# First mixer of a hybrid encoder: u's first block between the gate's two groups, LayerNorm's factor and shift behind the token mix, 1/sqrt for three blocks at once

## The chip, the cores and the metric

The kernel runs on one core of one Trainium2 chip. The metric is the time of one execution on the device, in microseconds (us); lower is better. The core has TensorE (matrix products, PE in the profile; its weight loads are PEld), VectorE (DVE), ScalarE (ACT), GpSimd (POOL) and SyncE (SP, which here issues nearly all transfers). They run side by side and wait for each other by semaphores.

## The reference

A trunk of two layers is applied to two token groups (512 and 256 tokens, width 1024) with shared weights. Layer 0 is half a SwiGLU block, a mixer, half a SwiGLU block; layer 1 the same with another mixer; a final RMSNorm follows. The change touches the mixer of layer 0:

```python
def layer_norm(x, g, b):
    x32 = x.astype(jnp.float32)
    mu = jnp.mean(x32, axis=-1, keepdims=True)
    var = jnp.mean(jnp.square(x32 - mu), axis=-1, keepdims=True)
    y = (x32 - mu) * lax.rsqrt(var + EPS)
    return y.astype(x.dtype) * g + b

def mixer_ab(h, w_in, sgu_ln_g, sgu_ln_b, sgu_w, sgu_b, sink, w_out):
    z = h @ w_in
    zs = jax.nn.gelu(z[..., :1024], approximate=False)
    u, vh = zs[..., :512], zs[..., 512:]
    vh = layer_norm(vh, sgu_ln_g, sgu_ln_b)
    vh = vh.reshape(B, nc, 128, 4, 128)
    vmix = jnp.einsum('gij,bnjgc->bnigc', sgu_w, vh) + jnp.transpose(sgu_b)[None, None, :, :, None]
    a_out = u * vmix.reshape(B, L, 512)
    ...
    b_out = window_gqa(rope_partial(q), rope_partial(k), v, sink)
    return jnp.concatenate([a_out, b_out], axis=-1) @ w_out
```

What is left out takes q, k and v from the other columns of z. So u is the multiplying half, vh the gate; the gate is normalised over its 512 columns for each token, mixed over the 128 tokens of a block with one matrix for each group of columns, and multiplied with u.

## The kernel before, in words

All 768 tokens are worked on together. The activations lie with the model's columns on partitions: eight tiles of 128 x 768. To keep float32 accuracy each operand of a product is split in a high part (a cast to fp32r, on ScalarE, `split` and `wsplit`, L193 and L111) and a low part (the rest, on VectorE, L194 and L112), and each product is three matmuls (`mm3`). Weights come in pieces of 512 KB through four "raw" buffers; a piece is split into "whi" and "wlo" tiles of 512 columns, of which there are five each (`NW`). PSUM is used as two pools of four banks: "mm" for projections, "aux" for all else.

The order on TensorE is written out by the program; the other engines' orders are planned when the kernel is built, by readiness and program order. What has to wait for other engines is written as generators ("chains"): each `yield x` says that the next step is due when x microseconds of matmul work, by the program's own count `self.t`, have been put behind it, and `tick` after every `mm3` runs the steps that are due. `drain` runs a chain to its end at once. So TensorE's order is fixed, and where a step's operand isn't ready TensorE stands still.

In `mixer0` (L916 and on) come, in this order: loads of tables; projections of keys and values; `attention` as a chain (12 units of scores, exps, transposes and products with the values, `score`, `turn`, `values`; L878, L883, L892, L141, L1051, L1055); query projections 0 to 2 (`q_heads`, with the rotation `roped`, L952 to L955); `vh_part`; query projection 3; `u_part`; and `mixer_out`, the output projection.

`vh_part` computes the gate in two groups of three token blocks, tokens on partitions, 512 columns on the free side, three "mm" banks at once; after a group three gelus (L1123) write "vg" tiles and a chain `sgu` is spawned for each block. `sgu` takes the statistics (L1084, L1087), forms 1/sqrt by `rsqrt` (13 operations on one column, L258 to L269), normalises (L1089), multiplies by g and adds b (L1092 and L1093, with both spread over the partitions); 8, 11 or 14 us later it splits (vhh, vhl), 4 us later it issues 12 matmuls for the token mix into an "aux" bank and adds the bias (L1107), which leaves the result with columns on partitions in the tiles `ot`. `u_part` takes u's columns in four blocks of 128: projection for 512 and for 256 tokens, scaling (L1133), gelu (L1134), and the product with `ot` (L1137); in front of the first product all `sgu` chains are drained.

The tag "tmp" has three buffers of 128 x 512; the gate's vg tiles, u's tiles, the rotation's two (rt, ru), vf and the attention's copy tb (L1051) share them. Gelu and exp are in different tables of ScalarE, so that a load (ACT_TABLE_LOAD) stands between them.

Of the kernel before, what the change touches and what calls it, by code (L numbers as in the profile page):

```python
# [21 lines left out]
TA, TB = 512, 256  # L22
T = TA + TB
H = T // 2
GROUPS = ((0, TA), (TA, T))
# [24 lines left out]
class Trunk:  # L50
# [864 lines left out]
    def mixer0(self):  # L915
        nc = self.nc  # L916
        mp = self.mixer_open("m0")
        self.spawn(self.norm_r(mp, False))
        xs = (self.xh, self.xl)
        tmp = lambda name: mp.tile([P, TA], F32, tag="tmp", name=name, bufs=3)  # L920
        rct = mp.tile([P, T], F32, tag="rct", name="rct")
        rst = mp.tile([P, T], F32, tag="rst", name="rst")
        for t, i in ((rct, 0), (rst, 1)):
# [5 lines left out]
        nc.sync.dma_start(sink, self.aps["sink"].partition_broadcast(P))  # L929
        nsink = mp.tile([P, 8], F32, tag="nsink", name="nsink")  # L930
        nc.vector.tensor_scalar(out=nsink, in0=sink, scalar1=-1.0, scalar2=None, op0=ALU.mult)
        lng = mp.tile([P, 512], F32, tag="lng", name="lng")
        nc.sync.dma_start(lng, self.aps["ln_g"].partition_broadcast(P))
        lnb = mp.tile([P, 512], F32, tag="lnb", name="lnb")
        nc.sync.dma_start(lnb, self.aps["ln_b"].partition_broadcast(P))
        sb = mp.tile([P, 512], F32, tag="sb", name="sb")
        nc.sync.dma_start(sb, self.aps["sgu_b"].partition_broadcast(P))
        swr = tmp("swr")
# [1 line left out]
        swh = mp.tile([P, 4, P], F32R, tag="swh", name="swh")  # L940
        swl = mp.tile([P, 4, P], F32R, tag="swl", name="swl")
        self.split(swh.rearrange("p g j -> p (g j)"), swl.rearrange("p g j -> p (g j)"), swr)
        swap = [i ^ 8 if i < 16 else i for i in range(32)]

        def rope_tables():
            for t in (rct, rst):
                nc.vector.tensor_tensor(out=t, in0=t, in1=self.rt, op=ALU.mult)
# [25 lines left out]
        for g in (0, 1):  # L973
            c0, c1 = GROUPS[g]
            t = roped(pkv[g][0], c0, c1)
# [3 lines left out]
                out=vf[:, : c1 - c0], in0=pkv[g][1][:, : c1 - c0], in1=self.rt[:, c0:c1], op=ALU.mult  # L979
# [3 lines left out]
        ot = [self.otile(k) for k in range(KD)]  # L983
# [73 lines left out]
                        in0=po[0:64, c], in1=tb[:, c], op=ALU.add,  # L1057
                    )

        qheads, gates = [], []  # L1060

        def attention(gap):
            cur = None
# [14 lines left out]
            yield 1.0  # L1078
            values(*cur, tt)

        def sgu(n, v):

            bs = mp.tile([P, 6], F32, tag="bs", name="bs", bufs=2)
            nc.vector.bn_stats(out=bs, in_=v)  # L1084
            mv = mp.tile([P, 8], F32, tag="mv", name="mv", bufs=2)
            it = mp.tile([P, 1], I32, tag="mvi", name="mvi", bufs=2)
            nc.vector.bn_aggr(out=mv[:, 0:2], in_=bs)  # L1087
            self.rsqrt(mv[:, 2:3], mv[:, 1:2], 1.0, mv[:, 3:4], mv[:, 4:5], it)
            nc.vector.tensor_scalar(  # L1089
                out=v, in0=v, scalar1=mv[:, 0:1], scalar2=mv[:, 2:3], op0=ALU.subtract, op1=ALU.mult  # L1090
            )
            nc.vector.tensor_tensor(out=v, in0=v, in1=lng, op=ALU.mult)  # L1092
            nc.vector.tensor_tensor(out=v, in0=v, in1=lnb, op=ALU.add)  # L1093
            yield SGU[0] + n % 3 * SGU[1]
            vh = mp.tile([P, 512], F32R, tag="vhh", name="vhh", bufs=2)
            vl = mp.tile([P, 512], F32R, tag="vhl", name="vhl", bufs=2)
            self.split(vh, vl, v)
            yield SGU[2]
            ps = self.psum(self.aux, "aux")
            for g in range(4):  # L1100
                c = slice(g * P, (g + 1) * P)
                self.mmul(ps[:, c], vh[:, c], swh[:, g, :], True, False)
                self.mmul(ps[:, c], vh[:, c], swl[:, g, :], False, False)
                self.mmul(ps[:, c], vl[:, c], swh[:, g, :], False, True)
            for g in range(4):
                c = slice(g * P, (g + 1) * P)
                nc.vector.tensor_tensor(  # L1107
                    out=ot[g][:, n * P : (n + 1) * P], in0=ps[:, c], in1=sb[:, c], op=ALU.add
                )

        def vh_part():
            for n0 in (0, 3):
                ps = [self.psum() for _ in range(3)]
                for k in range(KD):
                    if k % 2 == 0:
                        w = self.unit("l0_w_in", k, 2, 512, 512)
                    for i in range(3):
                        a, b = (n0 + i) * P, (n0 + i + 1) * P
                        st = (self.xh[k][:, a:b], self.xl[k][:, a:b])
                        self.mm3(ps[i], st, w[k % 2], k == 0, k == KD - 1)  # L1120
                for i in range(3):
                    v = tmp("vg")
                    nc.scalar.activation(v, ps[i], AF.Gelu, scale=self.ry[:, n0 + i : n0 + i + 1])  # L1123
                    gates.append(self.spawn(sgu(n0 + i, v)))

        def u_part():
            for m in range(4):
                w = self.unit("l0_w_in", 0, KD, m * P, P)
                for g in (0, 1):
                    c0, c1 = GROUPS[g]  # L1130
                    ps = self.proj(w, xs, GROUPS[g])
                    u = tmp("ug")[:, : c1 - c0]
                    nc.vector.tensor_tensor(out=u, in0=ps[:, : c1 - c0], in1=self.rt[:, c0:c1], op=ALU.mult)  # L1133
                    nc.scalar.activation(u, u, AF.Gelu)  # L1134
                    for c in gates:
                        self.drain(c)
                    nc.vector.tensor_tensor(out=ot[m][:, c0:c1], in0=ot[m][:, c0:c1], in1=u, op=ALU.mult)  # L1137

        att = self.spawn(attention(GAP0))
        for m in range(3):  # L1140
            q_heads(m)
        vh_part()
        q_heads(3)
        u_part()
        self.mixer_out("l0_w_out", ot, att)

# [317 lines left out]
def gqa_mask():  # L1464
    q = np.arange(P)[:, None]
    rel = np.arange(3 * P)[None, :] - P - q
    return np.where(np.abs(rel) <= P, 0.0, -NEG).astype(np.float32)
# [13 lines left out]
def trace(nc, phases=PHASES):  # L1481

    aps = {}
    inp = lambda n, s: aps.__setitem__(n, nc.dram_tensor(f"in_{n}", s, F32, kind="ExternalInput").ap())
    inp("x", (KD, P, T))
    inp("w", (WTOTAL,))
    inp("gains", (P, KD * len(NORMS)))
    inp("rope", (2, P, TA))
    inp("gmask", (P, 3 * P))
    inp("nmask", (P, NMASK))  # L1490
    inp("sink", (8,))
    inp("ln_g", (512,))
    inp("ln_b", (512,))
    inp("sgu_b", (512,))
    inp("sgu_w", (P, 4, P))
    inp("rpb", (16, 15, RPB_W))
    aps["y"] = nc.dram_tensor("out_y", (KD, P, T), F32, kind="ExternalOutput").ap()
    with tile.TileContext(nc) as tc:
        with ExitStack() as ctx:
            t = Trunk(ctx, tc, aps, phases)  # L1500
            with tc.manual_schedule(engines={mybir.EngineType.PE}):
                t.build()
    return t.units


def layout(units, i):
    x = np.concatenate([i["x_prompt"][0], i["x_sample"][0]], axis=0)
    order = np.arange(512).reshape(2, 4, 64).transpose(1, 0, 2).reshape(512)
    w_in = i["l0_w_in"]
    i = {  # L1510
        **i,
        "l0_w_in": np.concatenate([w_in[:, :1024], w_in[:, 1024:1536][:, order], w_in[:, 1536:]], axis=1),
        "l0_w_out": np.concatenate([i["l0_w_out"][:512], i["l0_w_out"][512:][order]], axis=0),
    }
    w = np.zeros(WTOTAL, np.float32)
    off = 0
    for name, k0, nk, c0, n in units:
        size = P * nk * n
        w[off : off + size].reshape(P, nk, n)[...] = (
            i[name][k0 * P : (k0 + nk) * P, c0 : c0 + n].reshape(nk, P, n).transpose(1, 0, 2)  # L1520
        )
        off += size
    rpb = np.zeros((16, 15, RPB_W), np.float32)
    rpb[:, :, RPB_PAD : RPB_PAD + 31] = i["l1_rpb"]
    return {
        "in_x": np.ascontiguousarray(x.T).reshape(KD, P, T),
        "in_w": w,
        "in_gains": np.ascontiguousarray(np.concatenate([i[n].reshape(KD, P).T for n in NORMS], axis=1)),
        "in_rope": rope_tables(),
        "in_gmask": gqa_mask(),  # L1530
        "in_nmask": natten_masks(),
        "in_sink": np.ascontiguousarray(i["l0_sink"].reshape(2, 4).T.reshape(8)),
        "in_ln_g": np.ascontiguousarray(i["l0_sgu_ln_g"]),
        "in_ln_b": np.ascontiguousarray(i["l0_sgu_ln_b"]),
        "in_sgu_b": np.ascontiguousarray(i["l0_sgu_b"].reshape(512)),
        "in_sgu_w": np.ascontiguousarray(i["l0_sgu_w"].transpose(2, 0, 1)),
        "in_rpb": rpb,
    }
# [21 lines left out]
```

## Time and profile before

| what | us |
|---|---|
| median of three runs | 2659.05 |
| lowest, highest | 2657.87, 2660.11 |
| the profiled execution | 2661.16 |
| its span (first to last instruction) | 2659.4 |
| TensorE busy in the span | 2582.3 |
| VectorE busy | 2262.8 |
| ScalarE busy | 1371.3 |
| mean granted clock of TensorE | 0.987 |

The profile is of one execution, taken by the hardware. L and a number name the line of the kernel that issued an instruction; a name such as ps_mm<-xh,whi reads "output<-inputs". Matmuls overlap one another, so their starts say more than their lengths. An idle time is shown in brackets with what ended it; only idle time on the engine that sets the end costs time.

### The profile page before, as it was taken

To read this page: it belongs to the slowest core of one execution; us is meant where nothing else is said; L and a number is where in the kernel's file an instruction comes from. 1 tells how busy PE (TensorE), PEld (TensorE's weight loads), DVE (VectorE), ACT (ScalarE), POOL (GpSimd) and SP (SyncE) were. 2 spreads that over 40 slices of the span, in tenths; PEclk is the share of its full clock that TensorE was granted. 3 is DMA by queue.
4 is the path that set the end of the run, shared out by engine and by line. 5 is a ranking of instruction groups with operands and counts; after the bars stand their busy time and mean duration, and the time that the engine had idled before them with its cause. 6 is when DMAs were issued, how large, how long until landed. Compare 5 with 4: busy or idle time off the path is not lost.

```text
span 2659.4 us, 41163 instructions
## 1 busy us (share of the span) xinstructions
PE 2582.3 (97%) x15150; PEld 2513.1 (94%) x15150; DVE 2262.8 (85%) x4748; ACT 1371.3 (52%) x2847; POOL 82.7 (3%) x124
## 2 busy tenths in 40 slices
PE   7999999999999999999999999999999989999997
PEld 6999999977889999999999999988998989999997
DVE  8989889779869988898998888886667699888886
ACT  6545444555746544445654544454555465454443
POOL 0000000000100000000000000002112100000000
PEclk9999999999999999999999999999999999999999
DMA  5333222421222222222222222232221322222221
GB/s 163 118 81 106 71 72 64 156 74 37 84 80 80 80 78 65 80 72 88 80 80 80 64 80 64 82 123 64 62 62 44 100 88 80 80 71 73 67 86 55
DMA packets 82746, 214.80 MB, mean 81 GB/s; under 512 B 19952, under 2 KB 32752, under 8 KB 82544
## 3 DMA queue, kind: packets, MB, share of 16 engines
q1 hardware_dynamic: 82400, 212.14, 26.0%
q8 instruction: 119, 1.95, 0.3%
q14 instruction: 83, 0.68, 0.1%
q10 hardware_dynamic: 144, 0.03, 0.0%
HBM read 202.70 MB, written 15.07 MB: 82 GB/s over the span
## 4 chain that ended last, share of the span: by engine, by line
PE 91%; DVE 5%; ACT 3%; DMA 0%; issue 0%; SPq 0%; DVEq 0%; ACTq 0%
PE ps_mm L137 59%; PE ps_aux L137 32%; PE ps_aux L141 1%; DVE wlo L112 1%; DVE xl L710 1%; ACT whi L111 0%; DMA raw<-in_w 0%; ACT xh L709 0%; DVE x L677 0%; DVE ol L194 0%; ACT sq L216 0%; DVE x L632 0%; ACT p L883 0%; ACT diag L247 0%; DVE tmp L348 0%
## 5 line engine op out<-in xcount | busy, mean ns | idle before, releaser
L111 ACT CAST whi<-s 128x512 fp32r<-128x512 f32 x496 | 302.0, 620 | 378.5 <-DVE s L580 141.2
L111 ACT CAST whi<-raw 128x512 fp32r<-128x512 f32 x512 | 311.7, 618 | 272.4 <-PE ps_mm L137 135.9
L112 DVE TENSOR_TENSOR wlo<-s,whi 128x512 fp32r<-128x512 f32 x496 | 335.1, 685 | 73.2 <-ACT whi L111 72.9
L112 DVE TENSOR_TENSOR wlo<-raw,whi 128x512 fp32r<-128x512 f32 x494 | 336.7, 687 | 33.9 <-ACT whi L111 30.9
L137 PE MATMUL ps_aux<-dt,whi 128*128 128x384 f32 x864 | 221.5, 338 | 0.0
L137 PE MATMUL ps_mm<-db,whi 128*128 128x384 f32 x864 | 221.5, 338 | 0.0
L137 PEld LDWEIGHTS ps_mm<-db,whi 128*128 128x128 f32 x864 | 156.8, 188 | 0.0
L137 PEld LDWEIGHTS ps_aux<-dt,whi 128*128 128x128 f32 x864 | 156.8, 188 | 0.0
L137 PE MATMUL ps_mm<-xh,whi 128*128 128x512 f32 (+1 forms) x416 | 146.8, 353 | 3.0 <-ACT xh L709 3.0
L137 PE MATMUL ps_mm<-db,wlo 128*128 128x384 f32 x432 | 146.0, 338 | 0.0
L137 PE MATMUL ps_aux<-dt,wlo 128*128 128x384 f32 x432 | 146.0, 338 | 0.0
L137 PE MATMUL ps_mm<-xl,whi 128*128 128x512 f32 (+1 forms) x416 | 142.7, 343 | 1.1 <-DVE xl L710 1.1
L137 PE MATMUL ps_mm<-xh,wlo 128*128 128x512 f32 (+1 forms) x416 | 142.3, 342 | 0.0
L467 ACT COPY u<-ps_mm 128x384 f32<-128x384 f32 x176 | 83.6, 475 | 34.5 <-PE ps_mm L137 34.2
L472 DVE TENSOR_TENSOR u<-ps_aux,u 128x384 f32<-128x384 f32 x176 | 96.9, 551 | 5.0 <-PE ps_aux L137 3.9
L580 DVE TENSOR_TENSOR s<-raw,raw 128x512 f32<-128x512 f32 x124 | 83.3, 685 | 20.9 <-DMA raw<-in_w 20.9
L580 DVE TENSOR_TENSOR s<-raw 128x512 f32<-128x512 f32 x124 | 84.8, 685 | 17.2 <-DMA raw<-in_w 16.9
L137 PE MATMUL ps_aux<-dh,whi 128*128 128x384 f32 x384 | 98.5, 338 | 0.7 <-DVE x L677 0.7
L883 ACT ACTIVATE p<-p,st 128x256 f32<-128x256 f32 (+3 forms) x144 | 69.1, 481 | 53.3 <-DVE st L878 53.2
L632 DVE TENSOR_TENSOR x<-ps_aux,x 128x384 f32<-128x384 f32 x160 | 86.3, 552 | 10.9 <-PE ps_aux L137 10.8
L137 PE MATMUL ps_mm<-oh,whi 128*128 128x384 f32 x256 | 90.2, 352 | 5.1 <-DVE x L861 4.0
L137 PEld LDWEIGHTS ps_mm<-xh,whi 128*128 128x128 f32 x416 | 79.4, 191 | 14.2 <-ACT xh L709 4.1
(427 smaller groups left out, 8098.2 us busy)
## 6 DMA issues: line engine op xcount, KB each, us to landing
raw<-in_w SPq DMA_DIRECT2D x342, 512.0 KB, 3.7
xdm<-x SPq DMA_DIRECT2D x16, 384.0 KB, 2.3
x<-in_x SPq DMA_DIRECT2D x16, 192.0 KB, 5.7
x<-xdm SPq DMA_DIRECT2D x8, 384.0 KB, 3.6
xold<-xdm SPq DMA_DIRECT2D x8, 384.0 KB, 3.1
out_y<-y SPq DMA_DIRECT2D x8, 384.0 KB, 2.5
tab<-skew SPq DMA_DIRECT2D x8, 256.0 KB, 4.6
raw<-in_w SPq DMA_DIRECT2D x8, 256.0 KB, 2.6
```

What stands on the lines that cost most here:

```text
L111: nc.scalar.copy(hi, src)
L112: (eng or nc.gpsimd).tensor_tensor(out=lo, in0=src, in1=hi.bitcast(F32), op=ALU.subtract)
L137: self.nc.tensor.matmul(out, lhsT=lhsT, rhs=rhs, start=start, stop=stop, **kw)
L141: self.nc.tensor.transpose(out, src, self.ident)
L467: nc.scalar.copy(e[n, out], bank[key, n])
L472: nc.vector.tensor_tensor(out=t, in0=bank[key, n], in1=t, op=ALU.add)
L580: f = lambda o, x, y, op: self.nc.vector.tensor_tensor(out=o, in0=x, in1=y, op=op)
L632: nc.vector.tensor_tensor(out=o, in0=ps, in1=o, op=ALU.add)
L710: nc.vector.scalar_tensor_tensor(out=lo, in0=src, scalar=gain, in1=hi.bitcast(F32), op0=ALU.mult, op1=ALU.subtract)
L883: nc.scalar.activation(outs[i - n0], outs[i - n0], AF.Exp, scale=-1.0, bias=mn[:, i : i + 1], accum_out=sm[:, i : i + 1])
```

## The change

Four things are edited, all in the first mixer:

1. `u_gelu(m)` is the first part of u's block (projection, scaling, gelu), now apart from the product with `ot`. Block 0 is computed between the gate's first and second group; blocks 1 to 3 stay in `u_part`. The products of block 0 come with those of block 1, behind the drain, which now stands behind both projections of block 1. u gets tiles of its own, two for each token group.
2. LayerNorm's g and b leave the token-major side. As the token mix is linear, g multiplies its result, with a scalar for each partition (L1107 becomes a scalar_tensor_tensor), and b is folded with the row sums of the mixing matrix into the bias tile `sb`. The chain `shift`, due 14 us of matmul work after its start, does this: two matmuls of a matrix of ones with the split mixing matrices, and four operations on VectorE. Instead of two loads of 512 values for all partitions there is one of 128 x 8.
3. `stats` takes the statistics of three blocks and runs `rsqrt` once, on three columns; it stands after the three gelus.
4. The tag "tmp" has five buffers instead of three.

```diff
@@ -917,7 +917,7 @@
         mp = self.mixer_open("m0")
         self.spawn(self.norm_r(mp, False))
         xs = (self.xh, self.xl)
-        tmp = lambda name: mp.tile([P, TA], F32, tag="tmp", name=name, bufs=3)
+        tmp = lambda name: mp.tile([P, TA], F32, tag="tmp", name=name, bufs=5)
         rct = mp.tile([P, T], F32, tag="rct", name="rct")
         rst = mp.tile([P, T], F32, tag="rst", name="rst")
         for t, i in ((rct, 0), (rst, 1)):
@@ -929,10 +929,8 @@
         nc.sync.dma_start(sink, self.aps["sink"].partition_broadcast(P))
         nsink = mp.tile([P, 8], F32, tag="nsink", name="nsink")
         nc.vector.tensor_scalar(out=nsink, in0=sink, scalar1=-1.0, scalar2=None, op0=ALU.mult)
-        lng = mp.tile([P, 512], F32, tag="lng", name="lng")
-        nc.sync.dma_start(lng, self.aps["ln_g"].partition_broadcast(P))
-        lnb = mp.tile([P, 512], F32, tag="lnb", name="lnb")
-        nc.sync.dma_start(lnb, self.aps["ln_b"].partition_broadcast(P))
+        ln = mp.tile([P, 8], F32, tag="ln", name="ln")
+        nc.sync.dma_start(ln, self.aps["ln"])
         sb = mp.tile([P, 512], F32, tag="sb", name="sb")
         nc.sync.dma_start(sb, self.aps["sgu_b"].partition_broadcast(P))
         swr = tmp("swr")
@@ -941,6 +939,19 @@
         swl = mp.tile([P, 4, P], F32R, tag="swl", name="swl")
         self.split(swh.rearrange("p g j -> p (g j)"), swl.rearrange("p g j -> p (g j)"), swr)
         swap = [i ^ 8 if i < 16 else i for i in range(32)]
+
+        def shift():
+            yield 14.0
+            ps = self.psum(self.aux, "aux")
+            for i, t in enumerate((swh, swl)):
+                self.mmul(ps, self.onesr, t.rearrange("p g j -> p (g j)"), i == 0, i == 1)
+            for g in range(4):
+                c = slice(g * P, (g + 1) * P)
+                nc.vector.scalar_tensor_tensor(
+                    out=sb[:, c], in0=ps[:, c], scalar=ln[:, 4 + g : 5 + g], in1=sb[:, c], op0=ALU.mult, op1=ALU.add
+                )
+
+        self.spawn(shift())
 
         def rope_tables():
             for t in (rct, rst):
@@ -1057,7 +1068,7 @@
                         in0=po[0:64, c], in1=tb[:, c], op=ALU.add,
                     )
 
-        qheads, gates = [], []
+        qheads, gates, us = [], [], {}
 
         def attention(gap):
             cur = None
@@ -1078,19 +1089,23 @@
             yield 1.0
             values(*cur, tt)
 
-        def sgu(n, v):
-
-            bs = mp.tile([P, 6], F32, tag="bs", name="bs", bufs=2)
-            nc.vector.bn_stats(out=bs, in_=v)
-            mv = mp.tile([P, 8], F32, tag="mv", name="mv", bufs=2)
-            it = mp.tile([P, 1], I32, tag="mvi", name="mvi", bufs=2)
-            nc.vector.bn_aggr(out=mv[:, 0:2], in_=bs)
-            self.rsqrt(mv[:, 2:3], mv[:, 1:2], 1.0, mv[:, 3:4], mv[:, 4:5], it)
+        def stats(vs):
+
+            mv = mp.tile([P, 5, 3], F32, tag="mv", name="mv", bufs=2)
+            it = mp.tile([P, 3], I32, tag="mvi", name="mvi", bufs=2)
+            for i, v in enumerate(vs):
+                bs = mp.tile([P, 6], F32, tag="bs", name="bs", bufs=2)
+                nc.vector.bn_stats(out=bs, in_=v)
+                nc.vector.bn_aggr(out=mv[:, 0:2, i], in_=bs)
+            self.rsqrt(mv[:, 2, :], mv[:, 1, :], 1.0, mv[:, 3, :], mv[:, 4, :], it)
+            return mv
+
+        def sgu(n, v, mv):
+
+            i = n % 3
             nc.vector.tensor_scalar(
-                out=v, in0=v, scalar1=mv[:, 0:1], scalar2=mv[:, 2:3], op0=ALU.subtract, op1=ALU.mult
+                out=v, in0=v, scalar1=mv[:, 0, i : i + 1], scalar2=mv[:, 2, i : i + 1], op0=ALU.subtract, op1=ALU.mult
             )
-            nc.vector.tensor_tensor(out=v, in0=v, in1=lng, op=ALU.mult)
-            nc.vector.tensor_tensor(out=v, in0=v, in1=lnb, op=ALU.add)
             yield SGU[0] + n % 3 * SGU[1]
             vh = mp.tile([P, 512], F32R, tag="vhh", name="vhh", bufs=2)
             vl = mp.tile([P, 512], F32R, tag="vhl", name="vhl", bufs=2)
@@ -1104,12 +1119,15 @@
                 self.mmul(ps[:, c], vl[:, c], swh[:, g, :], False, True)
             for g in range(4):
                 c = slice(g * P, (g + 1) * P)
-                nc.vector.tensor_tensor(
-                    out=ot[g][:, n * P : (n + 1) * P], in0=ps[:, c], in1=sb[:, c], op=ALU.add
+                nc.vector.scalar_tensor_tensor(
+                    out=ot[g][:, n * P : (n + 1) * P], in0=ps[:, c], scalar=ln[:, g : g + 1], in1=sb[:, c],
+                    op0=ALU.mult, op1=ALU.add,
                 )
 
         def vh_part():
             for n0 in (0, 3):
+                if n0:
+                    u_gelu(0)
                 ps = [self.psum() for _ in range(3)]
                 for k in range(KD):
                     if k % 2 == 0:
@@ -1118,23 +1136,31 @@
                         a, b = (n0 + i) * P, (n0 + i + 1) * P
                         st = (self.xh[k][:, a:b], self.xl[k][:, a:b])
                         self.mm3(ps[i], st, w[k % 2], k == 0, k == KD - 1)
+                vs = []
                 for i in range(3):
-                    v = tmp("vg")
-                    nc.scalar.activation(v, ps[i], AF.Gelu, scale=self.ry[:, n0 + i : n0 + i + 1])
-                    gates.append(self.spawn(sgu(n0 + i, v)))
+                    vs.append(tmp("vg"))
+                    nc.scalar.activation(vs[i], ps[i], AF.Gelu, scale=self.ry[:, n0 + i : n0 + i + 1])
+                mv = stats(vs)
+                for i in range(3):
+                    gates.append(self.spawn(sgu(n0 + i, vs[i], mv)))
+
+        def u_gelu(m):
+            w = self.unit("l0_w_in", 0, KD, m * P, P)
+            for c0, c1 in GROUPS:
+                ps = self.proj(w, xs, (c0, c1))
+                u = us[m, c0] = mp.tile([P, c1 - c0], F32, tag=f"ug{c0}", name="ug", bufs=2)
+                nc.vector.tensor_tensor(out=u, in0=ps[:, : c1 - c0], in1=self.rt[:, c0:c1], op=ALU.mult)
+                nc.scalar.activation(u, u, AF.Gelu)
 
         def u_part():
-            for m in range(4):
-                w = self.unit("l0_w_in", 0, KD, m * P, P)
-                for g in (0, 1):
-                    c0, c1 = GROUPS[g]
-                    ps = self.proj(w, xs, GROUPS[g])
-                    u = tmp("ug")[:, : c1 - c0]
-                    nc.vector.tensor_tensor(out=u, in0=ps[:, : c1 - c0], in1=self.rt[:, c0:c1], op=ALU.mult)
-                    nc.scalar.activation(u, u, AF.Gelu)
-                    for c in gates:
-                        self.drain(c)
-                    nc.vector.tensor_tensor(out=ot[m][:, c0:c1], in0=ot[m][:, c0:c1], in1=u, op=ALU.mult)
+            for m in range(1, 4):
+                u_gelu(m)
+                for c in gates:
+                    self.drain(c)
+                for c0, c1 in GROUPS:
+                    for k in (0, 1) if m == 1 else (m,):
+                        u = us[k, c0]
+                        nc.vector.tensor_tensor(out=ot[k][:, c0:c1], in0=ot[k][:, c0:c1], in1=u, op=ALU.mult)
 
         att = self.spawn(attention(GAP0))
         for m in range(3):
...
@@ -1530,8 +1555,7 @@
-        "in_ln_g": np.ascontiguousarray(i["l0_sgu_ln_g"]),
-        "in_ln_b": np.ascontiguousarray(i["l0_sgu_ln_b"]),
+        "in_ln": np.ascontiguousarray(np.concatenate([i[f"l0_sgu_ln_{n}"].reshape(4, P).T for n in "gb"], axis=1)),
```

More of the change, by code (lines that the diff above doesn't have):

```diff
@@ L1491, in trace @@
     inp("sink", (8,))
-    inp("ln_g", (512,))
-    inp("ln_b", (512,))
+    inp("ln", (P, 8))
     inp("sgu_b", (512,))
```

## The prediction

> **What bounds the kernel now.** I read the page first, for the engine shares.
>
> ```profile
> span 2659.4 us, 41163 instructions
> PE 2582.3 (97%) x15150; PEld 2513.1 (94%) x15150; DVE 2262.8 (85%) x4748; ACT 1371.3 (52%) x2847; POOL 82.7 (3%) x124
> ```
>
> TensorE is busy for 97% of the span, so the kernel can only get shorter where TensorE stands still or runs slowly, or where its work shrinks. The change takes no matmul out. All that can be won is therefore idle time and slow clock inside the first mixer. The windows view gives the part of it that holds the gate and u in stretches; the columns are the stretch, its length, then busy time with instruction count for each engine, the granted TensorE clock, the DMA share and GB/s.
>
> ```profile
> core 0: us, PE busy (x) PEld busy (x) DVE busy (x) ACT busy (x) POOL busy (x), PEclk, DMA share, GB/s
> 590.00:595.00 5.00, 4.54 (x22) 2.98 (x20) 3.43 (x15) 4.58 (x10) 0.00 (x0) 1.00 0.00 0
> 595.00:600.00 5.00, 1.79 (x7) 1.17 (x8) 4.57 (x21) 4.94 (x9) 0.00 (x0) 1.00 0.35 105
> 600.00:605.00 5.00, 5.00 (x22) 4.47 (x21) 4.94 (x26) 2.01 (x4) 0.00 (x0) 0.66 0.00 0
> 605.00:630.00 25.00, 24.32 (x157) 20.56 (x156) 22.72 (x81) 14.11 (x35) 0.00 (x0) 1.00 0.21 65
> 635.00:640.00 5.00, 5.00 (x41) 4.59 (x42) 5.00 (x32) 4.10 (x11) 0.00 (x0) 1.00 0.00 0
> 640.00:645.00 5.00, 4.25 (x25) 3.56 (x24) 5.00 (x23) 1.77 (x3) 0.00 (x0) 1.00 0.00 2
> 645.00:650.00 5.00, 2.95 (x21) 2.54 (x21) 5.00 (x17) 1.94 (x4) 0.00 (x0) 1.00 0.00 0
> 650.00:655.00 5.00, 2.90 (x13) 2.93 (x14) 4.95 (x16) 1.38 (x3) 0.00 (x0) 0.65 0.01 3
> 655.00:660.00 5.00, 5.00 (x26) 3.74 (x26) 3.73 (x15) 1.58 (x7) 0.00 (x0) 0.67 0.01 2
> 660.00:710.00 50.00, 47.35 (x307) 40.20 (x307) 40.36 (x120) 42.32 (x84) 2.54 (x2) 1.00 0.22 66
> ```
>
> There are two holes. The first, at 595 to 600, has ACT full (4.94 of 5); the second, at 640 to 655, has DVE full (5.00 of 5). After each hole the clock is down to about two thirds over a five-microsecond stretch. The order of time on TensorE says what ended them (start, duration, what it is, in brackets the idle time before it and who ended it).
>
> ```profile
> 595.07 0.50 PE L137 MATMUL ps_mm<-whi,xh 128*128 128x512 f32 x1 [0.53 <-ACT vg L1123]
> 595.41 0.40 PE L137 MATMUL ps_mm<-wlo,xh 128*128 128x512 f32 x1
> 595.64 0.40 PE L137 MATMUL ps_mm<-whi,xl 128*128 128x512 f32 x1
> 599.18 0.50 PE L137 MATMUL ps_mm<-whi,xh 128*128 128x512 f32 x1 [3.14 <-ACT vg L1123]
> 602.31 0.63 PE L137 MATMUL ps_mm<-whi,xh 128*128 128x512 f32 x1
> 602.74 0.63 PE L137 MATMUL ps_mm<-wlo,xh 128*128 128x512 f32 x1
> 616.07 0.22 PE L137 MATMUL ps_aux<-swh,vhh 128*128 128x128 f32 x1
> 645.09 0.33 PE L137 MATMUL ps_aux<-swh,vhl 128*128 128x128 f32 x1 [0.84 <-DVE vhl L194]
> 652.10 0.45 PE L137 MATMUL ps_aux<-swh,vhh 128*128 128x128 f32 x1 [4.05 <-DVE o L1055]
> ```
>
> **Stall A** (0.53 + 3.14 = 3.67 us): the gate's second group of three blocks needs three "mm" PSUM banks; there are four, and the first group's three stay taken until their gelus have read them. **Stall B** (0.84 + 4.05 = 4.89 us): the token mix of blocks 3 and 4 waits, first for a split of the normalised gate, then for an "aux" bank that the attention's values still hold. Matmuls of 512 columns start every 0.23 us at 595.41 and 595.64, but every 0.43 us at 602.31 and 602.74. A clock of 0.66 over 5 us costs 1.7 us at 600 to 605; 0.65 and 0.67 cost 1.75 and 1.65 us after B, less the 0.3 us or so of the first that fell in the idle time: 3.1 us. Together A costs 3.67 + 1.7 = 5.4 us and B costs 4.89 + 3.1 = 8.0 us; 13.4 us in all.
>
> The Trainium skill, "TensorE: Matmul & The Clock Gate", section "What's actually happening", says that the array falls to half clock after an idle window of about 3.4 us and needs a busy window as long to recover. The rows agree in size, although here a wait of 3.14 us was enough. By that rule a shorter remaining wait costs no clock; the sum below does not use this.
>
> **The change, part by part.**
>
> *u's first block between the groups.* It puts 24 matmuls of 512 columns and 24 of 256 there. At 0.23 us each, and half of that for 256 (an estimate from the same rows), this is 8.3 us of TensorE work, taken from behind the last query projection, so nothing is added. Its first projection takes the fourth, free bank; its second needs, 5.5 us later, only the bank of the first gelu. The group behind it needs the other two gelu banks at about 603 us.
>
> ```profile
> 598.44 1.27 ACT L1123 ACTIVATE vg<-ps_mm,sm 128x512 f32<-128x512 f32 x2
> 649.76 0.58 ACT L1051 COPY tb<-ps_aux 64x512 f32<-64x512 f32 x1
> L111 ACT CAST whi<-raw 128x512 fp32r<-128x512 f32 x21 | 12.5, 617 | 8.4 <-PE ps_mm L137 7.9 <-POOL wlo L112 0.5
> ```
>
> Those two gelus ended at 599.7 us in this trace, so A goes whole: -5.4 us. What could uncover it is u's weights; the last row shows that the casts of weights wait for TensorE to free one of five buffers, so they run ahead, and this cover holds. If it failed, half of A would stay (2.7 us).
>
> *Factor and shift behind the token mix; one 1/sqrt for three blocks; five "tmp" buffers.* These act on B. By groups (busy, mean ns):
>
> ```profile
> L1092 DVE TENSOR_TENSOR vg<-vg,lng 128x512 f32<-128x512 f32 x6 | 4.1, 688 | 0.0
> L1093 DVE TENSOR_TENSOR vg<-vg,lnb 128x512 f32<-128x512 f32 x6 | 4.1, 675 | 0.0
> L267 DVE TENSOR_TENSOR mv<-mv 128x1 f32<-128x1 f32 x18 | 2.6, 154 | 0.0
> L1107 DVE TENSOR_TENSOR o<-ps_aux,sb 128x128 f32<-128x128 f32 x24 | 5.7, 280 | 0.0
> L710 DVE SCALAR_TENSOR_TENSOR xl<-x,gains,xh 128x384 fp32r<-128x384 f32 x16 | 9.8, 615 | 0.5 <-ACT xh L709 0.5
> L632 DVE TENSOR_TENSOR x<-ps_aux,x 128x384 f32<-128x384 f32 x8 | 4.4, 549 | 0.4 <-PE ps_aux L137 0.4
> ```
>
> The two passes go: 8.2 us. Of six chains of 13 small operations, two stay; 52 operations at 154 ns are 8.0 us, or about half of that where they overlap: 4. L1107 becomes an operation with a per-partition scalar; L710 against L632 prices that at 66 ns, 24 times, 1.6 us. So VectorE loses 10.6 us, half of it, 5.3, in front of each group's token mix, and the shift adds four operations like L1107, 1.1 us, with the key and value projections beside them: nothing on the path; uncovered it would be 1.1.
>
> B's long wait follows from this load and from the buffers:
>
> ```profile
> 645.70 0.74 DVE L952 STREAM_SHUFFLE ru<-ps_mm 128x512 f32<-128x512 f32 x1
> ```
>
> The last rotation of queries (L952) starts only when the gate's splits free two of three "tmp" buffers, and the copy of the values (the L1051 row above, 649.76) needs one too. With five buffers the three gate tiles leave two free. VectorE was full from 635 to 655; taking 5.3 us from what stands before 652.1 moves that point to 646.8, ahead of 648.05 (652.10 less 4.05), where TensorE asked; the 0.84 us goes likewise. So B goes: -8.0 us. But the margin is 1.2 us, and VectorE remains nearly full there, so I keep 1.5 us back. The bounds are 0 and 4.9 (all of B's waiting stays), as other full stretches lose little: 0.68 us in the 25 us from 605.
>
> *The added wait.* The merged chain starts when all three gelus are done; the normalisations, splits and token mix of block 0 queue behind it. Its length is bounded by two chains of before, first operation and first normalisation of each:
>
> ```profile
> 595.99 0.15 DVE L258 TENSOR_SCALAR mv<-mv 128x1 f32<-128x1 f32 x1
> 598.84 0.55 DVE L1089 TENSOR_SCALAR vg<-vg,mv 128x512 f32<-128x512 f32 x1
> 601.89 0.14 DVE L258 TENSOR_SCALAR mv<-mv 128x1 f32<-128x1 f32 x1
> 609.33 0.54 DVE L1089 TENSOR_SCALAR vg<-vg,mv 128x512 f32<-128x512 f32 x1
> 615.67 0.69 DVE L194 TENSOR_TENSOR vhl<-vg,vhh 128x512 fp32r<-128x512 f32 x1
> ```
>
> Alone it takes 2.9 us, mixed with other work 7.4 us. Gelus end at 599.7, the statistics last until 601.9 as here, then come the chain, 0.5 us to normalise and 1.3 us to split (a cast of 617 ns and the L194 row's 0.69): block 0 is ready between 606.6 and 611.1. TensorE asks at 616.07 less the 5.4 us of A, 610.7, since its order counts matmul time, and u's block only takes the place of other matmuls. So the cost is 0 to 0.4 us as computed, more if the splits queue; I take 1.0, between 0 and 5.7 (the last under the rivals). In the second group the three gelus already stood together, so the chain there only gets shorter.
>
> *The shift's two matmuls* of 512 columns are new on TensorE: 2 x 0.23 = 0.5 us. *DMA:* two loads leave SP's queue in front of the spatial weights, a smaller one comes.
>
> ```profile
> L933 SPq DMA_DIRECT2D lng<-in_ln_g x1: 432/432/432, 526.5 to 526.5; - x1
> ```
>
> An issue is 0.43 us; the spatial weights are used long after, so I take 0, between -0.4 and +0.4. *Multiplications by u:* same eight, the first two later, with the second u projection's end beside them; uncovered, 0.6 us each. *End of the stage:* 2.65 us idle in 660 to 710 comes from u's last block meeting the attention's exps and the output's splits; TensorE's order there is unchanged, so it stays.
>
> **Sum:** -5.4 - 8.0 + 1.5 + 1.0 + 0.5 = -10.4 us. The profiled execution took 2661.16 us (span 2659.4 and 1.8 around it), 2.1 above the median of 2659.05; it would take 2650.8. On the median, 2648.6.
>
> **The rivals.**
>
> 1. *Only A goes.* VectorE stays the bound near 645, and the bank is as late as now. For: VectorE was full for 15 us. Against: the 5.3 us taken away. Time: -5.4 + 0.5 + about 0.4 = -4.5, so 2654.5.
>
> 2. *Tables.* u's gelus land among the attention's exps.
>
> ```profile
> L1134 ACT ACT_TABLE_LOAD x6 | 7.7, 1283 | 0.4 <-DVE st L890 0.3
> L1123 ACT ACT_TABLE_LOAD x3 | 3.8, 1283 | 0.1
> ```
>
> Two more switches there and back are four loads, 5.1 us, in a queue that is full at 595 to 600, while copies and splits for TensorE wait behind. Half of it uncovered: 2.6 us, 2651.2. Against: ACT is busy 2.01 of 5 right behind, and the gelus are moved, not added. The Trainium skill, "ScalarE: Activation LUTs", section "Table sets: the hidden batching unit", tells to finish one table set before the next, and the page counts 2.66 us a switch; the first gelu starts 1.3 us after its load here, so the trace has half. By the page's price this rival would be at about 2654.
>
> 3. *Slower: the merged chain is late for the fixed order.* If it takes as long as block 1 did, from its gelu's end at 599.7 to the end of its split at 616.4, 16.7 us, block 0 is 5.7 us late. TensorE waits in front of it, and the clock falls again for 1.7. Twice, once per group: 14.8 us against 12.9 won, +2, and up to +6 where the slow clock lasts as it did after B. It begins to cost from a chain of 11 us and decides from about 16. Against: block 1's time holds two passes that are gone and a due time, not need. Time: 2661 to 2665.
>
> 4. *It does nothing: the holes only move,* because ACT or VectorE bounds the stage as a whole. Against: from 660 to 710 they are busy for 42.3 and 40.4 of 50, not all. Time: 2657 to 2660.
>
> **How the numbers follow.** Forecast 0.62 (its own range 2645.6 to 2652), rival 1 0.14, rival 2 0.10, rival 3 0.08, rival 4 0.06. About 0.2%, 5.3 us, can be told from no change. Faster: 0.62, nine tenths of rival 2 and a quarter of rival 1, 0.75. Slower: over half of rival 3, 0.05. Same: the rest, 0.20. The range reaches from 2644 (13.4 us and some of the stage's end) to 2656, past rival 1; rivals 3 and 4, 0.14, are left out.
>
> **What would show it.** A: no wait for vg in front of the second group, the clock 1.00 there, u's matmuls behind the first gelus. B: no wait for L1055's successor above 1 us, L952 soon after its projection. Chain: waits for the gate's splits below 1 us. It is wrong if either stretch still shows a clock near 0.66, if a new wait for vhh or vhl exceeds 3 us, or if the stage after 700 us grows by more than 2.

## The result, and the profile after

The changed kernel takes 2651.24 us (median of six, 2644.97 to 2652.09) beside 2658.46 for the kernel before: a ratio of 0.9966, 95% interval 0.9956 to 0.9976. In a second comparison it took 2651.50 beside 2659.28: 0.9973 (0.9963 to 0.9984). So it saves 7 to 8 us, 0.3%, which is clear of the measurement. The forecast was 10.4 us and 2648.6.

The page of the changed kernel's first profiled execution begins:

```profile
span 2643.2 us, 41100 instructions
PE 2572.0 (97%) x15152; PEld 2505.8 (95%) x15152; DVE 2254.0 (85%) x4688; ACT 1368.7 (52%) x2845; POOL 82.6 (3%) x124
```

This execution took 2644.97 us, the shortest of its six. It is not the typical one, and the difference of 16.2 us to the profiled execution of before must not be read as the gain; the section on the hardware says what else is in it.

The windows view of the first mixer, with the columns as in the prediction, shows both holes closed and a new one behind them:

```profile
595.00:600.00 5.00, 5.00 (x31) 4.32 (x30) 3.30 (x13) 4.33 (x8) 0.00 (x0) 1.00 0.11 43
600.00:605.00 5.00, 4.69 (x42) 4.22 (x41) 4.94 (x22) 4.66 (x10) 0.00 (x0) 1.00 0.01 3
615.00:620.00 5.00, 4.03 (x31) 3.56 (x32) 4.97 (x19) 3.24 (x9) 0.00 (x0) 1.00 0.52 202
640.00:660.00 20.00, 19.29 (x133) 16.52 (x132) 19.82 (x67) 11.25 (x24) 0.00 (x0) 1.00 0.08 27
600.00:680.00 80.00, 77.77 (x498) 65.97 (x497) 71.12 (x233) 54.88 (x114) 2.56 (x2) 1.00 0.16 50
680.00:700.00 20.00, 15.78 (x103) 14.71 (x102) 16.35 (x45) 16.43 (x37) 1.28 (x1) 0.91 0.44 145
```

TensorE is idle for 2.23 us from 600 to 680, at full clock. Between 640 and 660 VectorE is still full (19.82 of 20), but TensorE waits for only 0.71 us there, where the kernel before waited for 4.89. From 680 to 700, where the projections of u end and the output projection begins, it is idle for 4.22 us, and the clock is down for a part of it. The list of TensorE's waits from 592 to 720 (total, times, longest) names the cause, and the order of time on TensorE, ScalarE and VectorE shows how it arises:

```profile
PE ps_aux L137 <- DVE tl L194: 4.8, 3, 4.2
PE ps_aux L137 <- DVE o L1122: 1.2, 1, 1.2
```

```profile
685.98 0.34 PE L137 MATMUL ps_mm<-oh,wlo 128*128 128x384 f32 x1
686.15 1.47 PE L141 MATMUL ps_aux<-ident,p 128*128 128x128 f32 x12
692.72 0.38 PE L137 MATMUL ps_aux<-kh,qh 64*128 64x256 f32 x1 [4.22 <-DVE tl L194]
```

```profile
687.08 3.39 ACT L193 CAST oh<-o 128x384 fp32r<-128x384 f32 x8
690.49 1.56 ACT L193 CAST th<-ps_aux 128x512 fp32r<-128x512 f32 x3
```

```profile
687.77 4.30 DVE L194 TENSOR_TENSOR ol<-o,oh 128x384 fp32r<-128x384 f32 x9
691.99 1.87 DVE L194 TENSOR_TENSOR tl<-ps_aux,th 128x512 fp32r<-128x512 f32 x3
```

TensorE has put the attention's transposes into "aux" banks and wants the next bank for scores. It comes free when the transposes are split (th, tl). Their splits stand behind eight casts and nine subtractions for the output projection (oh, ol). All twelve splits of the output projection are issued when it is opened. Here the transposes (L141) come only behind its first three matmuls, so in program order the twelve stand in front of th and tl.

In the kernel before, the transposes of the same attention unit stood inside u's last projection, in front of the output projection:

```profile
695.54 0.28 PE L137 MATMUL ps_mm<-xh,wlo 128*128 128x256 f32 x1
695.66 1.47 PE L141 MATMUL ps_aux<-ident,p 128*128 128x128 f32 x12
698.32 0.38 PE L137 MATMUL ps_aux<-kh,qh 64*128 64x256 f32 x1 [0.51 <-DVE tl L194]
```

```profile
697.57 1.89 DVE L194 TENSOR_TENSOR tl<-ps_aux,th 128x512 fp32r<-128x512 f32 x3
699.37 0.55 DVE L194 TENSOR_TENSOR ol<-o,oh 128x384 fp32r<-128x384 f32 x1
```

There th and tl went in front of all output splits but one, and the scores behind them waited for 0.51 us. So the change has turned the order on TensorE at this place. That u's move is what turned it is shown by e1 and e2 below. How it does so is read from the program and not tested: the attention's steps come by pace, and with one block of u in front of the last query projection, less of u is left to run beside the attention's later units.

### The profile page after: what moved, and what is told of

Read it like the earlier page. It is cut to its first block, busy times and chain, and to the rows that moved or that the text cites. A ratio compares the mean times of both kernels' runs of the same rounds, so it can differ in the third digit from the quotient of the medians.

```text
span 2643.2 us, 41100 instructions
## 1 busy us (share of the span) xinstructions
PE 2572.0 (97%) x15152; PEld 2505.8 (95%) x15152; DVE 2254.0 (85%) x4688; ACT 1368.7 (52%) x2845; POOL 82.6 (3%) x124
## 4 chain that ended last, share of the span: by engine, by line
PE 90%; DVE 6%; ACT 3%; issue 1%; DMA 0%; SPq 0%; DVEq 0%; ACTq 0%
PE ps_mm L137 58%; PE ps_aux L137 31%; PE ps_aux L141 1%; DVE wlo L112 1%; DVE xl L710 1%; ACT whi L111 1%; DVE ol L194 0%; DMA raw<-in_w 0%; ACT xh L709 0%; DVE x L632 0%; DVE x L677 0%; ACT sq L216 0%; DVE tl L194 0%; DVE s L580 0%; DVE p L878 0%
## 5 line engine op out<-in xcount | busy, mean ns | idle before, releaser
L580 DVE TENSOR_TENSOR s<-raw 128x512 f32<-128x512 f32 x124 | 84.8, 685 | 16.5 <-DMA raw<-in_w 16.2
L632 DVE TENSOR_TENSOR x<-ps_mm,x 128x384 f32<-128x384 f32 x160 | 86.9, 550 | 6.0 <-PE ps_mm L137 5.9
```

The lines of the kernel that those rows point to most:

```text
L580: f = lambda o, x, y, op: self.nc.vector.tensor_tensor(out=o, in0=x, in1=y, op=op)
L632: nc.vector.tensor_tensor(out=o, in0=ps, in1=o, op=ALU.add)
```

## The experiments

Times are medians; ratios are to the kernel before, measured on the same chip in between. There were three rounds, with medians of the kernel before of 2659.28 (the first, e1, e2, e4), 2659.17 (e3, e5, e6, e7) and 2658.47 us (e8, e9, e10), so times of different rounds can differ by 0.8 us for no other reason. "Idle" is TensorE's idle time between 640 and 660 us, "clock" its granted clock there, both from the windows view of one execution of each (4.89 and 0.83 before, 0.71 and 1.00 after).

| kernel | us | ratio (95%) | idle | clock |
|---|---|---|---|---|
| changed kernel, again | 2651.50 | 0.9973 (0.9963 to 0.9984) | 0.43 | 1.00 |
| e1: without u's move | 2653.40 | 0.9978 (0.9969 to 0.9986) | 1.50 | 1.00 |
| e2: u's move alone | 2660.44 | 1.0005 (0.9996 to 1.0014) | 7.07 | 0.77 |
| e3: five tmp buffers alone | 2657.91 | 0.9998 (0.9989 to 1.0007) | 2.76 | 0.70 |
| e4: changed, late half | 2646.37 | 0.9956 (0.9944 to 0.9969) | 0.43 | 1.00 |
| e5: factor and shift alone | 2656.23 | 0.9991 (0.9982 to 1.0000) | 2.90 | 0.83 |
| e6: changed, 1/sqrt for each block | 2654.66 | 0.9985 (0.9976 to 0.9994) | 2.51 | 0.83 |
| e7: before, late half | 2656.87 | 0.9993 (0.9984 to 1.0002) | 4.89 | 0.83 |
| e8: e1 and late half | 2652.03 | 0.9975 (0.9965 to 0.9984) | 1.49 | 1.00 |
| e9: changed, three tmp buffers | 2656.67 | 0.9992 (0.9983 to 1.0000) | 4.36 | 0.91 |
| e10: e5 and e3 together | 2653.04 | 0.9980 (0.9971 to 0.9989) | 1.75 | 1.00 |

### The changed kernel, again

The same file, for a second trace.

> The changed kernel itself, for a second trace. Theory (the runs differ by how long the clock of TensorE stays low, not by their waits): 2650 to 2652 us again, the waits of TensorE between 590 and 700 us as in the first trace within 0.5 us (2.2 us up to 680, then one of about 4.2 for a split of the transposes), and 4 to 7 us more of slow clock somewhere, in steps of about 1.7. Rival (the first mixer itself runs differently from one execution to the next): the waits between 590 and 700 differ by over 3 us and the clock elsewhere is the same.

It took 2651.50. The wait at the end is the same to the hundredth:

```profile
694.78 0.58 PE L137 MATMUL ps_aux<-kh,qh 64*128 64x256 f32 x1 [4.22 <-DVE tl L194]
```

```profile
600.00:680.00 80.00, 77.81 (x494) 66.20 (x492) 70.31 (x230) 52.86 (x111) 2.56 (x2) 0.98 0.16 48
680.00:700.00 20.00, 15.78 (x92) 14.26 (x91) 15.70 (x43) 18.44 (x41) 1.28 (x1) 0.83 0.46 155
```

TensorE waits as long as in the first trace (2.19 and 4.22 us against 2.23 and 4.22). Its clock is lower: 0.98 against 1.00, which is 1.6 us of 80, and 0.83 against 0.91, 1.6 us of 20. The rival, that the mixer itself waits differently, falls. To weigh the mixer alone, one can measure it from the first gelu of the gate to the last addition of the output projection (L826). Each row gives the first and the last start; the pairs are of the kernel before, the first and the second trace of the changed one:

```profile
L1123 ACT ACTIVATE vg<-ps_mm,sm x6: 680/687/691, 594.3 to 632.3; 128x512 f32<-128x512 f32 x6
L826 DVE TENSOR_TENSOR x<-ps_mm,x x16: 547/558/559, 710.3 to 786.7; 128x384 f32<-128x384 f32 x16
```

```profile
L1142 ACT ACTIVATE vg<-ps_mm,sm x6: 679/688/690, 592.9 to 637.4; 128x512 f32<-128x512 f32 x6
L826 DVE TENSOR_TENSOR x<-ps_mm,x x16: 546/557/559, 697.5 to 775.2; 128x384 f32<-128x384 f32 x16
```

```profile
L1142 ACT ACTIVATE vg<-ps_mm,sm x6: 679/688/690, 593.3 to 639.4; 128x512 f32<-128x512 f32 x6
L826 DVE TENSOR_TENSOR x<-ps_mm,x x16: 550/558/559, 700.4 to 778.0; 128x384 f32<-128x384 f32 x16
```

That is 192.4 us before, 182.3 and 184.7 after: 10.1 and 7.7 us less.

### e1: the changed kernel without u's move

```diff
             for n0 in (0, 3):
-                if n0:
-                    u_gelu(0)
...
-            for m in range(1, 4):
+            for m in range(4):
                 u_gelu(m)
...
-                    for k in (0, 1) if m == 1 else (m,):
+                    for k in (m,):
```

> The changed kernel with u's first block back behind the last query projection; everything else of the change stays. Theory (two stalls, removed by two separate parts): the first stall of 3 to 4 us, ended by the gelus, and its slow clock come back, 5.4 us slower than the changed kernel, about 2656; the second stall stays gone. Rival 1 (VectorE's relief alone does it, as the gelus come earlier): within 1.5 us of the changed kernel. Rival 2 (u's move is what relieves the second stretch too): both stalls come back, 2659 or more.

2653.40, 1.9 us slower than the changed kernel, a difference that the two intervals don't separate. The waits are those of the theory, the time is not: it is near the first rival's, though stall A is back.

```profile
PE ps_mm L137 <- ACT vg L1140: 3.7, 2, 3.2
PE ps_aux L137 <- DVE vhl L194: 1.3, 1, 1.3
PE ps_mm L137 <- DVE ol L194: 1.0, 2, 0.8
```

Stall A is back with its 3.7 us, stall B is gone. But the wait of 4.2 us for tl at the end of the stage is gone too: without u's move it never arises. So u's move wins A and gives most of it back 90 us later.

### e2: u's move alone

The kernel before with `u_gelu` between the groups, u's own tiles and the later products; the rest as before.

> The kernel before with u's first block between the groups and tiles of its own for u, nothing else changed (three tmp buffers, factor and shift on the gate, 1/sqrt per block). Theory: the first stall goes, the second stays: 5.4 us faster than before, about 2653. Rival (the normalised gate is then late for the first group too, with VectorE as loaded as before): a new wait for vhl in the first group takes back half or more, 2656 to 2660.

2660.44: no gain. The rival was right in its size, but not in its place: the new wait is not for the first group.

```profile
PE ps_aux L137 <- ACT qh L909: 6.9, 1, 6.9
PE ps_aux L137 <- DVE tl L194: 5.2, 4, 4.2
```

Stall A is gone, and two waits have come: 6.9 us for the split of the rotated queries, which with VectorE full (20.00 of 20 between 640 and 660) and three tmp buffers are late, and the wait of 4.2 us for tl at the end. The second shows that u's move brings that wait in either kernel: here too the transposes come behind the first matmuls of the output projection, while in e1 and e10 they stand inside u's last projection, as before.

### e4: the changed kernel, the second half's output splits issued later

```diff
         for k in early:
-            ready(k)
+            ready(k, HALVES if cols else HALVES[:1])
...
-                put(m, h, self.proj(w, src, HALVES[h], ks=early))
+                ps = self.proj(w, src, HALVES[h], ks=early)
+                if not (cols or m or h):
+                    for k in early:
+                        ready(k, HALVES[1:])
+                put(m, h, ps)
```

The first output projection reads only the first 384 tokens. `ready` now splits those alone before it, and the other half behind it in program order, so that the attention's splits stand in between.

> The changed kernel, but in the output projection the splits of the second half of the tokens are issued behind the first projection instead of with those of the first half, so that the attention's splits (th, tl) stand in front of them. Theory (the forecast's step that the end of the stage stays was wrong: a wait of 4.2 us with its slow clock of 1.7 has taken the place of 2.65 us): the wait for tl falls below 1.5 us and the time by 3 to 5 us against the changed kernel, to about 2647. Rival (VectorE and ScalarE are simply full at the end of the stage, twelve splits take what they take): the wait moves to the output's splits, and the time is within 1.5 us of the changed kernel.

2646.37, 5.1 us faster than the changed kernel in the same comparison and 0.44% faster than before: the fastest version here.

```profile
689.79 1.56 ACT L193 CAST th<-ps_aux 128x512 fp32r<-128x512 f32 x3
691.23 2.59 ACT L193 CAST oh<-o 128x384 fp32r<-128x384 f32 x6
```

```profile
680.00:700.00 20.00, 18.54 (x117) 17.16 (x116) 16.47 (x45) 18.63 (x40) 1.29 (x1) 0.91 0.28 87
```

The th casts now go in front of six of the oh casts, and the idle time of this stretch is 1.46 us in place of 4.22. ScalarE is at least as busy as in the changed kernel (18.63 of 20 beside 16.43 and 18.44 in its two traces) and TensorE waits less: what was wrong was the order of the work, not its amount.

### e7 and e8: the late half without u's move

e7 is the same edit on the kernel before, e8 on e1.

> The kernel before with the output's splits of the second half of the tokens behind the first output projection, nothing else. Theory (this order is worth much only where the twelve splits stand ready together, as in the changed kernel, where it gave 5 us): 0 to 2.5 us faster than before, from the 2.65 us idle at the end of the stage. Rival (it is worth the same anywhere): 4 to 6 us faster.

> The changed kernel with u's first block back behind the last query projection (as e1_no_u) and the late second half of the output's splits (as e4_late_half). It completes a square: with both splits' orders, u's move there or not. Theory (u's move is worth the whole first stall, 5 us or so, and the wait that it brings at the end of the stage hides 3 to 4 of it): without u's move the late half gives little, 0 to 2 us against e1_no_u, so 2651 to 2653, and u's move with it is worth 5 to 6 (2646.4 against this). Rival (the late half is a gain of its own, 5 us, and u's move is worth 2 us either way): 2648 to 2649.

e7 gave 2656.87 beside 2659.17, and the interval of its ratio just includes no change; e8 gave 2652.03, 1.4 us less than e1, which is within the uncertainty. With e1, the changed kernel and e4 this is a square: u's move is worth 1.9 us with the old order of the splits (2653.4 to 2651.5) and 5.7 us with the new one (2652.0 to 2646.4; 6.5 us if each is taken against the kernel before in its own round), the latter close to the 5.4 us at which stall A was priced. The rival, a gain of its own, falls.

### e3, e5, e10: what closes stall B

e3 has five tmp buffers and nothing else, e5 the shift chain, L1122's form and no passes for g and b, e10 both.

> The kernel before with five tmp buffers instead of three, nothing else. Theory (the second stall is a matter of buffers: the copy of the attention's values and the rotation wait for a tile that the gate holds): the wait of 4.05 us goes with most of its slow clock, 4 to 7 us faster than before, 2652 to 2655; the first stall of 3.7 stays. Rival (it is VectorE's load, and a tile more only changes the order in which a full engine works): the idle time between 640 and 660 stays over 3 us, within 2 us of before.

> The kernel before with LayerNorm's factor and shift behind the token mix (the two passes gone, the shift's chain added), three tmp buffers, 1/sqrt per block, u where it was. Theory of load (VectorE is full from 635 to 655, 3.6 us of passes go in front of the second token mix): the wait of 4.05 falls below 1.5, 4 to 7 us faster than before. Theory of buffers: three gate tiles still hold all three buffers until they are split, the wait falls only by as much as the splits come earlier, 1 to 2.5 us, and the time by 1 to 3.

> The kernel before with two of the parts, factor and shift behind the token mix and five tmp buffers; 1/sqrt per block, u where it was. Theory (the second stall has two causes, each of which is enough to keep it, so that each part alone gave nothing or 3 us): together they take the idle time between 640 and 660 from 4.9 to below 1.5 us with its slow clock, 5 to 7 us faster than before, 2652 to 2654, as e1_no_u without its merged 1/sqrt. Rival (the merged 1/sqrt is needed too, as it was worth 3 us in the changed kernel): the idle time there stays over 2 us, 2655 to 2657.

TensorE's longest waits in the stage (592 to 720) without A, e3 first, then e5:

```profile
PE ps_aux L137 <- DVE vhl L194: 2.8, 2, 2.6
```

```profile
PE ps_aux L137 <- ACT th L193: 2.9, 1, 2.9
```

Each part alone takes the idle time of 4.89 us to just under 3. With the buffers alone the rotation starts early (at 640.09 us instead of 645.70) on a full VectorE, and the gate's splits are late instead (vhl). With VectorE relieved alone the bank's release still comes late. The times say less: e3 is within 1.3 us of before, e5 2.9 us below it. The clock column shows one reason: what either part left was still followed by the slow clock (0.70 and 0.83), as stall B was (0.83). Together (e10) they leave 1.75 us at full clock and gain 5.4. So stall B had two causes, each of which keeps a good half of it. The theory for e10 held in its time (2652 to 2654); its bound of 1.5 us of idle time was missed by 0.25.

### e6 and e9: one part of the changed kernel taken back

e6 forms 1/sqrt in the loop over blocks, e9 has `bufs=3` for tmp.

> The changed kernel with 1/sqrt formed for each block again (39 small operations per group instead of 13), all else as changed. Theory (the merged chain is worth little once passes and buffers are gone, as the three chains interleave): within 2 us of the changed kernel. Rival 1 (VectorE is still nearly full, 26 operations more at 0.07 to 0.15 us per group bring the second stall back): 3 to 6 us slower than the changed kernel, new waits for vhl. Rival 2 (the merged chain makes block 0 wait for the last gelu): the wait of 1.2 us near 616 goes, 1 to 2 us faster.

> The changed kernel with three tmp buffers as before, all else as changed. Theory (three gate tiles hold all three buffers from their gelus to their splits, so the rotation of queries and the copy of the attention's values wait, as in e2_u_only): a wait of 4 to 7 us comes back near 650, 5 to 9 us slower than the changed kernel, 2656 to 2660. Rival (VectorE's relief alone was enough, the two more buffers do nothing, as they did by themselves): within 2 us of the changed kernel.

e6: 3.2 us slower than the changed kernel, with a new wait for the rotated queries. e9: 5.2 us slower, with the same wait, longer.

```profile
PE ps_aux L137 <- ACT qh L909: 2.5, 1, 2.5
```

```profile
PE ps_aux L137 <- ACT qh L909: 4.0, 1, 4.0
```

In e6 (the first row) 52 small operations more bring back 2.5 us of waiting at 648: VectorE has no room to spare there in the changed kernel (19.82 of 20), so that work put in front of the second token mix comes out as a wait, though not for vhl, as the rival had it. The wait near 616 stayed at 0.9, so the merged chain does not cost there. e9 confirms the buffers: with three, the rotation (L963) starts at 647.85 instead of 641.60, behind the gate's splits.

## Why the prediction was right in kind and its gain 3 us too large

**Stall A** goes, as forecast: TensorE is busy for 5.00 of 5 us from 595 to 600 at a clock of 1.00. **Stall B** goes, as forecast and for the reasons given, load and buffers; e10 shows that both were needed. The merged 1/sqrt counts where u's block stands in front of it (e6: 2.51 us idle beside 0.43). Without u's move no gain by it is seen: e1, which has it (and tiles of its own for u), leaves 1.50 us and takes 2653.40, e10 leaves 1.75 and takes 2653.04.

**The added wait** was forecast at 1.0 us, with the merged chain between 2.9 and 7.4. It took 6.8 us, from its first operation to the first normalisation:

```profile
599.43 0.15 DVE L258 TENSOR_SCALAR mv<-mv 128x3 f32<-128x3 f32 x1
606.27 1.44 DVE L1106 TENSOR_SCALAR vg<-vg,mv 128x512 f32<-128x512 f32 x3
607.71 0.68 DVE L194 TENSOR_TENSOR vhl<-vg,vhh 128x512 fp32r<-128x512 f32 x1
```

Block 0 was ready at 608.4, and its matmuls began without a wait at 608.6. TensorE came there 2 us earlier than the 610.7 reckoned, so this term was nearer than it looked: rival 3, the late chain, was 0.2 us from beginning to cost, but far from the 5.7 us at which it was priced. What TensorE waited for instead was an "aux" bank held by L1122, 1.2 us. With the 2.5 us kept back for the chain and VectorE's fullness, and the 0.68 us left in place from 605 on, the forecast allowed 3.2 us of waiting in the gate's stretch; it was 2.2.

**L1107's new form** was priced at 66 ns more; it went from 280 to 343, 63 more:

```profile
L1122 DVE SCALAR_TENSOR_TENSOR o<-ps_aux,ln,sb 128x128 f32<-128x128 f32 x24 | 6.8, 343 | 0.1
```

**Tables** (rival 2): loads around the stage (560 to 740) fell from 19 to 17, where more were feared, since u's gelus are moved next to the gate's.

```profile
L883 ACT ACT_TABLE_LOAD x9 | 11.5, 1283 | 0.2
L1153 ACT ACT_TABLE_LOAD x5 | 6.4, 1283 | 0.1
L1142 ACT ACT_TABLE_LOAD x3 | 3.8, 1283 | 0.1
```

**The step that failed** is the last of the sum: "*End of the stage:* 2.65 us idle in 660 to 710 comes from u's last block meeting the attention's exps and the output's splits; TensorE's order there is unchanged, so it stays." It was not unchanged. The attention's transposes, which stood inside u's last projection before (695.66), come behind the first matmuls of the output projection after (686.15), and with them the order of ScalarE and VectorE turned: the output's splits went ahead of the attention's. The 2.65 us became 4.22, with 1.8 us (first trace) or 3.4 us (second) of slow clock, which there was none of before: 3.4 to 5.0 us more. Less the 1.0 us of waiting that was allowed for in the gate's stretch and didn't come, that is 2.4 to 4.0; the forecast gain was 2.6 to 3.2 too large. e4 takes this away and lands at 2646.4, 2.2 below the forecast. None of the signs of being wrong that the prediction named looked at this place, and none of them appeared.

## What to carry to other kernels

Where one engine's order is written out and chains are put into it by pace, moving a block forward shifts each chain against all that follows: ask for every chain which of its steps will now fall behind other work in program order, and issue in program order only what the next consumer needs. Parts that look independent may gain only together: here three of them alone (e2, e3, e5) gave between nothing and 3 us, and each left or brought waits long enough for the clock to fall between 640 and 660. Weigh such a change by the waits in the stage in question, which repeated to a few hundredths in the two traces of the changed kernel, not by one execution's time.

## What the runs showed of the hardware that was not expected

The changed kernel's two traces have the same waits and spans of 2643.2 and 2650.0 us; what differs is how often the clock of TensorE falls. Over the whole span TensorE is idle for 71.2 us in the first (2643.2 less 2572.0 busy) and 71.6 in the second (2650.0 less 2578.4), so of the 6.8 us between them 6.4 lie in matmuls that ran slower; the mean granted clock is 0.991 and 0.988. The kernel before was idle for 77.1 us at 0.987: of the 16.2 us between the profiled executions, 5.9 are waiting. The plainest place has nothing to do with the change. In both traces TensorE is idle for 1.61 us between 865 and 870, most of it one wait for a cast of weights; in the first (upper fence) the clock stays, in the second it drops behind the wait.

```profile
865.00:870.00 5.00, 3.39 (x18) 2.75 (x17) 4.95 (x9) 1.93 (x4) 0.00 (x0) 1.00 0.31 93
870.00:875.00 5.00, 5.00 (x31) 5.00 (x30) 5.00 (x10) 4.28 (x9) 0.00 (x0) 1.00 0.41 120
```

```profile
865.00:870.00 5.00, 3.39 (x18) 2.75 (x17) 4.95 (x10) 1.93 (x4) 0.00 (x0) 1.00 0.16 19
870.00:875.00 5.00, 5.00 (x22) 5.00 (x21) 4.48 (x9) 2.65 (x5) 0.00 (x0) 0.66 0.55 173
```

0.66 over 5 us is 1.7 us lost, as after stall A. The wait of 1.2 us near 616 shows the same: from 605 to 630 the clock is 1.00 in the first trace and 0.93 in the second. So at these two places a wait of this size is a draw with a price of about 1.7 us. The Trainium skill, "TensorE: Matmul & The Clock Gate", section "What's actually happening", says that the activity window of 3.4 us runs freely and isn't set by the kernel's start. That fits the draw. It also says that the clock falls after a full idle window; here 1.61 us of idle time were enough, and the measurement decides.

The two stalls of before were no draw in the traces here. Behind stall A the clock fell in all seven that have it (before, e1, e3, e5, e7, e8, e10), by 1.7 us in six of them and about 3.4 in e5. Between 640 and 660 it fell in all seven with 2.5 us of idle time or more, and in none of the six with 1.75 or less. So, as far as these traces show, the 4.8 us of slow clock were as much a part of the gain as the 3.7 and 4.9 us of waiting in front of them.
